# Rotary embedding over eight batches: batch 3's store on sync, another share of TensorE tiles, a last batch stored in halves

## The chip, the cores and the metric

The kernel runs on one core of a Trainium2 chip. The metric is the device time of one execution in microseconds, as the median of several runs. The profile is one further execution taken by the hardware profiler; its span runs from the core's first instruction to its last, and is a little shorter than the device time.

## The reference

```python
x1 = x[..., : d_head // 2]
x2 = x[..., d_head // 2 :]
out1 = x1 * cos - x2 * sin
out2 = x1 * sin + x2 * cos
return np.concatenate([out1, out2], axis=-1)
```

`x` is 8 batches x 2048 positions x 8 heads x 64 values in float32 (33.55 MB); `cos` and `sin` are 2048 x 32 and shared by batches and heads. Every value of `x` is read once and every result written once, 67 MB in all, for two multiplications and one addition each.

## The kernel before

**Tiling.** A batch is one tile `xt` of 128 partitions x 8192 values: partition q holds 16 consecutive positions of 512 values (H x D). It is loaded as one DMA of 4 MB, in rows of 32 KB, and batch 0 as rows of 8, 8 and 16 KB. Five such tiles are there (`NBUF = 5`); results are written over the input in the same tile, and the tile is stored from there. Batches 0 to 4 are loaded at the start; batch b + 5 is loaded by `load` after batch b has been stored, into the tile that this frees.

**Pieces.** A batch is worked on in four pieces of 2048 values per partition (`UNIT`); the first batch begins with two half pieces, and the last ends with two. Each piece is one call of `rotate`, in one of three kinds, which `kinds` (L98 to L100) sets:
- A (the default): GpSimd makes `t2`, the sin products with halves swapped, in two instructions (L122). VectorE makes `t1 = x * cos` (L129), and adds `t1 + t2` into `xt` (L136).
- B: GpSimd and VectorE make `t2` and `t1` as in A, but TensorE adds them: it multiplies both by the unit matrix `eye` and accumulates in PSUM (L143, L144), in two halves `o`, and ScalarE copies each half into `xt` (L145).
- C: GpSimd has no part. VectorE makes the cos product (L129) and the sin product (L148); TensorE adds or subtracts them by `eye` and `neye` (L160, L161), and ScalarE copies (L165).

Before the change, the first piece of batches 1 and 3 is C, the first of 2, 4 and 5 is B, and all others are A.

**Buffers.** `t2` of A and B pieces comes from a pool of three buffers, `t1` of A pieces from one buffer in PSUM, `t1` of B pieces and both products of C pieces from a pool of two (`t1s`), and `o` from one PSUM buffer. A buffer is used again when its last reader is done: for `t2` that is VectorE's addition in an A piece and TensorE's last matmul in a B piece. Which buffer a tile gets is settled when the program is built.

**Order and queues.** `keep` holds the instructions of each engine in the order of the source. There are two DMA queues in use: loads are issued by sync (SP), stores by scalar (ACT), apart from the last batch, whose stores sync issues after its last load. A queue issues in order, and an issue waits until what it reads is computed or what it overwrites is stored. Batch 0 is stored as rows of 2, 14 and 16 KB, the last batch as rows of 16, 8 and 8 KB (`shares`), and every other batch as one DMA of 4 MB.

Of the kernel before, what the change touches and what calls it, by code (L numbers as in the profile page):

```python
# [10 lines left out]
def kernel(  # L11
# [7 lines left out]
    nc = tc.nc  # L19
# [4 lines left out]
    B, S, H, D = x.shape  # L24
# [5 lines left out]
    UNIT = 4 * HD  # L30
    NBUF = 5
    C = 512
    last = B - 1
# [36 lines left out]
        xts[b] = xt  # L70

    def store(b, lo, n):
        queue = nc.sync if b == last else nc.scalar
        keep(queue.dma_start(out=ov[b, :, lo : lo + n], in_=xts[b][:, lo : lo + n]))

    keep(nc.scalar.dma_start(out=sin_sb, in_=sin_src))
# [19 lines left out]
        return dataclasses.replace(a, ap=[a.ap[0][:], a.ap[1][:], [0, n], a.ap[-1][:]])  # L96

    kinds = {}  # L98
    for b, kind in ((1, "C"), (2, "B"), (3, "C"), (4, "B"), (5, "B")):
        kinds[(b, 0)] = kind  # L100

    def rotate(b, lo, n):
        kind = kinds.get((b, lo), "A")
# [73 lines left out]
    def shares(b):  # L177
        if b == 0:
            return [HD, 7 * HD, 2 * UNIT]
        if b == last:  # L180
            return [2 * UNIT, UNIT, UNIT]
        return [ROW]

    for b in range(B):
        done = 0
        outs = list(spans(shares(b)))
        for lo, n in spans(pieces(b)):
            rotate(b, lo, n)
            done = lo + n
            while outs and sum(outs[0]) <= done:  # L190
                store(b, *outs.pop(0))
        if b + NBUF <= last:
            load(b + NBUF)
# [30 lines left out]
```

## Time and profile before

| | us |
|---|---|
| median of 3 runs (lowest to highest) | 163.42 (163.29 to 163.53) |
| span of the profiled execution | 161.6 |
| VectorE busy | 140.1 (87%) |
| GpSimd busy | 138.9 (86%) |
| TensorE matmul busy | 47.1 (29%) |
| ScalarE busy | 12.8 (8%) |
| moved by DMA | 67.65 MB, 419 GB/s on average |

Of the profile's parts, the 40 slices give each engine's busy share in tenths over 40 equal parts of the span; the DMA row is the mean over the 16 DMA engines, which all queues share. The queue table gives each queue's share of the engines' time: q1 is sync's and q10 is scalar's. The timeline lists instructions with start, duration, engine (PE is TensorE, DVE VectorE, ACT ScalarE, POOL GpSimd, SP sync; a q behind the name marks a DMA issue) and line, and in brackets how long the engine was idle before it and what ended that.

The DMA issues, from the page: what, by which engine, how many, KB each and the median us from issue to landing:

| | count | KB | us to landing |
|---|---|---|---|
| loads by sync | 7 | 4096 | 40.3 |
| stores by scalar | 6 | 4096 | 28.3 |
| last batch's first store by sync | 1 | 2048 | 11.1 |
| last batch's two other stores by sync | 2 | 1024 | 7.5 |

### The profile page before, as it was taken

The page shows a single profiled execution, that of the slowest core. Times are in us where ns is not written, and L with a number is a line of the kernel's source. Part 1 is how long each engine was busy: PE and PEld are TensorE (multiplying, and loading weights), DVE is VectorE, ACT ScalarE, POOL GpSimd, SP SyncE. Part 2 cuts the span into 40 slices and gives each one's busy share as a digit, 9 for nine tenths or more (in the row PEclk, how much of TensorE's full clock was granted, in tenths as well). Part 3 has the DMA queues.
Part 4 walks back from the last instruction along what each step waited for, and adds up shares of the span by engine and source line. Part 5 has one row for each costly group of instructions (what it writes and reads, how often), then busy time and mean ns, then how long its engine had stood idle before and what let it go on. Part 6 is the DMA issues. An engine that isn't in the chain of part 4 may idle for free.

```text
span 161.6 us, 460 instructions
## 1 busy us (share of the span) xinstructions
PE 47.1 (29%) x80; PEld 17.8 (11%) x80; DVE 140.1 (87%) x66; ACT 12.8 (8%) x14; POOL 138.9 (86%) x70
## 2 busy tenths in 40 slices
PE   0000000597209750977039813972000000000000
PEld 0000000143004210322023302330000000000000
DVE  0297999999999999999999999699969999899920
ACT  3300000002200220022000120022000000000000
POOL 1399999999999999976999989997899979999500
PEclk9999999999965997599858995699555555555555
DMA  5999999999999999999999999999999999999995
GB/s 157 419 462 413 424 469 403 394 457 457 410 402 450 442 470 389 454 454 389 470 438 389 471 432 389 462 446 398 446 448 406 430 462 406 430 462 397 414 408 225
DMA packets 3458, 67.65 MB, mean 419 GB/s; under 512 B 384, under 2 KB 384, under 8 KB 768
## 3 DMA queue, kind: packets, MB, share of 16 engines
q1 hardware_dynamic: 2016, 38.01, 55.3%
q10 hardware_dynamic: 1440, 29.62, 42.9%
q14 instruction: 2, 0.02, 0.0%
HBM read 34.08 MB, written 33.55 MB: 419 GB/s over the span
## 4 chain that ended last, share of the span: by engine, by line
DVE 53%; DMA 29%; POOL 9%; issue 5%; DVEq 0%; SPq 0%; POOLq 0%
DVE t L129 28%; DMA xt<-in_x_dram 25%; DVE xt L136 22%; POOL t L122 9%; DMA sin_sb<-in_sin_dram 4%; DVE t L148 3%; DVEq L136 0%; SPq L67 0%; POOLq L122 0%
## 5 line engine op out<-in xcount | busy, mean ns | idle before, releaser
L122 POOL TENSOR_TENSOR t<-xt,sin_sb 128x1024 f32<-128x1024 f32 (+1 forms) x32 | 70.5, 2202 | 12.1 <-DMA xt<-in_x_dram 6.7
L129 DVE TENSOR_TENSOR t<-xt,cos_ps 128x2048 f32<-128x2048 f32 (+1 forms) x34 | 73.4, 2166 | 0.8
L122 POOL TENSOR_TENSOR t<-xt,nsin 128x1024 f32<-128x1024 f32 (+1 forms) x32 | 70.5, 2202 | 0.0
L136 DVE TENSOR_TENSOR xt<-t,t 128x2048 f32<-128x2048 f32 (+1 forms) x29 | 62.2, 2144 | 6.7 <-POOL t L122 4.1
L143 PE MATMUL o<-t,eye 128*128 128x512 f32 x24 | 15.9, 749 | 24.4 <-DVE t L129 21.0
L160 PE MATMUL o<-t,eye 128*128 128x512 f32 x16 | 11.2, 789 | 38.3 <-DVE t L129 36.1
L144 PE MATMUL o<-t,eye 128*128 128x512 f32 x24 | 14.7, 698 | 0.0
L145 ACT COPY xt<-o 128x1024 f32<-128x1024 f32 x6 | 6.1, 1012 | 45.7 <-PE o L144 45.7
L143 PEld LDWEIGHTS o<-t,eye 128*128 128x128 f32 x24 | 5.3, 247 | 33.6 <-issue 27.7
L160 PEld LDWEIGHTS o<-t,eye 128*128 128x128 f32 x16 | 3.7, 256 | 43.8 <-POOL t L122 30.2
L165 ACT COPY xt<-o 128x1024 f32<-128x1024 f32 x4 | 4.0, 1012 | 47.3 <-PE o L161 47.3
L93 DVE COPY cos_ps<-cos_sb 128x512 f32<-128x512 f32 x1 | 0.7, 694 | 7.0 <-DMA cos_sb<-in_cos_dram 7.0
L144 PEld LDWEIGHTS o<-t,eye 128*128 128x128 f32 x24 | 5.4, 227 | 7.4 <-issue 7.4
L161 PE MATMUL o<-t,neye 128*128 128x512 f32 x8 | 6.2, 863 | 0.2 <-DVE t L148 0.2
L148 DVE TENSOR_TENSOR t<-xt,sin_ps 128x2048 f32<-128x2048 f32 x2 | 4.6, 2280 | 0.0
L161 PE MATMUL o<-t,eye 128*128 128x512 f32 x8 | 4.1, 592 | 0.0
L161 PEld LDWEIGHTS o<-t,neye 128*128 128x128 f32 x8 | 1.8, 260 | 4.7 <-issue 3.0
L161 PEld LDWEIGHTS o<-t,eye 128*128 128x128 f32 x8 | 1.5, 190 | 1.9 <-issue 1.9
L90 ACT ACT_TABLE_LOAD x1 | 1.3, 1283 | 1.2 <-PEq L208 1.2
L90 ACT ACTIVATE nsin<-sin_sb 128x512 f32<-128x512 f32 x1 | 0.6, 630 | 4.1 <-DMA sin_sb<-in_sin_dram 4.1
L91 ACT COPY sin_ps<-sin_sb 128x512 f32<-128x512 f32 x1 | 0.6, 579 | 0.0
L80 POOL MEMSET eye<- 128x128 f32 x1 | 0.2, 205 | 0.3 <-POOLq L208 0.3
(6 smaller groups left out, 1.0 us busy)
## 6 DMA issues: line engine op xcount, KB each, us to landing
xt<-in_x_dram SPq DMA_DIRECT2D x7, 4096.0 KB, 40.3
out_dram<-xt ACTq DMA_DIRECT2D x6, 4096.0 KB, 28.3
xt<-in_x_dram SPq DMA_DIRECT2D x2, 1024.0 KB, 6.7
xt<-in_x_dram SPq DMA_DIRECT2D x1, 2048.0 KB, 12.4
out_dram<-xt ACTq DMA_DIRECT2D x1, 2048.0 KB, 25.9
out_dram<-xt SPq DMA_DIRECT2D x1, 2048.0 KB, 11.1
out_dram<-xt SPq DMA_DIRECT2D x2, 1024.0 KB, 7.5
out_dram<-xt ACTq DMA_DIRECT2D x1, 1792.0 KB, 20.8
```

The costliest lines, as they stand in the source:

```text
L90: keep(nc.scalar.mul(nsin, sin_sb, -1.0))
L93: keep(nc.vector.tensor_copy(cos_ps, cos_sb))
L122: nc.gpsimd.tensor_mul(out=t2u[:, :, u, :].rearrange("p (r h) d -> p r h d", h=H), in0=xu[:, :, 1 - u, :].rearrange("p (r h) d -> p r h d" ...
L129: nc.vector.tensor_mul(out=t1.rearrange("p (r k d) -> p r k d", r=nr, d=Dh), in0=xk, in1=rep(cos_ps[:, r0 : r0 + nr, :], 2 * H),)
L136: keep(nc.vector.tensor_add(out=xt, in0=t1, in1=t2))
L143: nc.tensor.matmul(oc, eye, t1[:, cs], start=True, stop=False)
L144: nc.tensor.matmul(oc, eye, t2[:, cs], start=False, stop=True)
L145: keep(nc.scalar.copy(xt[:, 2 * j * C : 2 * (j + 1) * C], o))
L148: nc.vector.tensor_mul(out=t2.rearrange("p (r k d) -> p r k d", r=nr, d=Dh), in0=xk, in1=rep(sin_ps[:, r0 : r0 + nr, :], 2 * H),)
L160: nc.tensor.matmul(oc, eye, t1u[:, gs, u, :], start=True, stop=False)
L161: nc.tensor.matmul(oc, eye if u else neye, t2u[:, gs, 1 - u, :], start=False, stop=True)
L165: nc.scalar.copy(xu[:, :, u, :], o.rearrange("p (g d) -> p g d", d=Dh))
```

## The change

```diff
     def store(b, lo, n):
-        queue = nc.sync if b == last else nc.scalar
+        queue = nc.sync if b in (3, last) else nc.scalar
...
     kinds = {}
-    for b, kind in ((1, "C"), (2, "B"), (3, "C"), (4, "B"), (5, "B")):
-        kinds[(b, 0)] = kind
+    for b, j, kind in (
+        (1, 0, "C"),
+        (2, 0, "C"),
+        (3, 0, "C"),
+        (4, 0, "B"),
+        (4, 2, "B"),
+        (5, 0, "B"),
+        (6, 0, "B"),
+    ):
+        kinds[(b, j * UNIT)] = kind
...
         if b == last:
-            return [2 * UNIT, UNIT, UNIT]
+            return [2 * UNIT, 2 * UNIT]
```

Three things change. Batch 3 is stored by sync; in the order of the source that store stands behind the load of batch 7, which is issued at the end of batch 2, so sync issues load 5, load 6, load 7, store 3 and then the last batch's stores. Seven pieces instead of five go through TensorE: three of kind C (batches 1, 2, 3) and four of kind B (batch 4's first and third, and the first of 5 and 6); batch 2's first piece turns from B to C. The last batch is stored as two DMAs of 16 KB rows; its second half of 2 MB, before two stores of 1 MB, each issued when its own piece was done, is now one store, issued when both are done.

## The prediction

> **What bounds the kernel now.** I read the 40 slices and the queue table first, then the timeline from 83 us on, then stretches around the first and the last transfer.
>
> The page's DMA row and queue table, then the stretches (length, busy time by engine, PE clock, DMA share, GB/s):
>
> ```profile
> DMA  5999999999999999999999999999999999999995
> ...
> q1 hardware_dynamic: 2016, 38.01, 55.3%
> q10 hardware_dynamic: 1440, 29.62, 42.9%
> ```
>
> ```profile
> 0.73:1.73 1.00, 0.00 (x0) 0.00 (x0) 0.00 (x0) 0.56 (x1) 0.49 (x2) 1.00 0.00 0
> 1.73:2.20 0.47, 0.00 (x0) 0.00 (x0) 0.00 (x0) 0.47 (x1) 0.00 (x0) 1.00 1.84 279
> ...
> 155.10:159.40 4.30, 0.00 (x0) 0.00 (x0) 0.00 (x0) 0.00 (x0) 0.00 (x0) 0.50 1.01 427
> 159.40:160.40 1.00, 0.00 (x0) 0.00 (x0) 0.00 (x0) 0.00 (x0) 0.00 (x0) 0.50 0.26 107
> ```
>
> The 16 DMA engines are full from 1.7 us to the last packet at 160.4 us; between them sync's queue (q1) and scalar's (q10) take 98%. So the transfers bound the kernel, and a change can gain only by fewer or shorter packets, and lose only by leaving the engines idle. The stretches also price an issue onto idle engines: the first load is issued at 0.73 and its first packets start between 1.73 and 2.20, so 1.0 us to the first engine and 1.5 us to the last.
>
> The timeline (start, duration, engine, line) shows the other runner, GpSimd with VectorE behind it:
>
> ```profile
> 85.49 2.29 DVE L136 TENSOR_TENSOR xt<-t,t 128x2048 f32<-128x2048 f32 x1
> ...
> 87.86 2.34 POOL L122 TENSOR_TENSOR t<-xt,sin_sb 128x1024 f32<-128x1024 f32 x1
> ...
> 92.36 1.02 PE L144 MATMUL o<-t,eye 128*128 128x512 f32 x2
> ...
> 93.42 1.01 ACT L145 COPY xt<-o 128x1024 f32<-128x1024 f32 x1 [3.79 <-PE o L144]
> 93.61 2.34 POOL L122 TENSOR_TENSOR t<-xt,sin_sb 128x1024 f32<-128x1024 f32 x1 [1.10 <-DMA xt<-in_x_dram]
> ...
> 113.71 2.34 POOL L122 TENSOR_TENSOR t<-xt,sin_sb 128x1024 f32<-128x1024 f32 x1 [1.69 <-DMA xt<-in_x_dram]
> ...
> 133.08 2.33 POOL L122 TENSOR_TENSOR t<-xt,sin_sb 128x1024 f32<-128x1024 f32 x1 [1.09 <-DMA xt<-in_x_dram]
> ...
> 144.77 10.24 SPq L74 DMA_DIRECT2D out_dram<-xt  x3
> ...
> 153.42 1.23 DVE L136 TENSOR_TENSOR xt<-t,t 128x1024 f32<-128x1024 f32 x1
> ```
>
> GpSimd works without a break from load to load and waits only 1.1 to 1.7 us at the head of a batch. Its last result reaches the last store at 154.67 (the third issue of the row at 144.77), and the engines drain at 160.4. So the compute chain is 2.2 us ahead of need: the second last store's packets run until 157.9, so the last could be issued as late as 157.9 - 1.0 = 156.9 before an engine goes idle.
>
> **The change, part by part.**
>
> *Last batch in two 2 MB stores.* By the packet records an 8 KB row takes 309 ns and a 16 KB row 611 ns. The last 2 MB are 16 rows of 8 KB per engine now (4.94 us) and 8 of 16 KB then (4.89): 0.06 us less. But nothing of the last 2 MB can start until both small pieces are done, where today its first half covers the wait for the second. All other transfers end at 160.4 - 4.94 = 155.4; so the last issue must come by 155.4 - 1.0 = 154.4. Each us after that is a us of idle engines.
>
> *Store 3 behind load 7.* SP issues it at about 92.9, right after load 7 (92.59); all it waits for is over by then. Nobody waits for it: loads 5, 6, 7 wait for stores 0, 1, 2. The two stores of batch 7 queue behind it on q1, but by 8 packets per engine, done near 132, when the first of them is 15 us away. q10 is empty from store 2's landing (92.5) until store 4, so loads 6 and 7 get up to double share and land near 104 and 114 to 122 (now 113.6 and 132.9). The engines stay full meanwhile, so this part costs and gains nothing by itself: it takes away GpSimd's waits of 1.69 and 1.09 us if GpSimd can use that. Fewer mixed loads and stores may help a little: 32 KB packets take 1213 ns in pure stretches and 1213 to 1221 on average in mixed ones, so at most 16 x 8 ns = 0.13 us.
>
> *Batch 2's piece as C.* One L148 multiply more on VectorE (2.2 us, as 62.45 to 80.90 for batch 3, 18.45 us, against 46.21 to 62.45 for batch 2, 16.24), 4.6 us less on GpSimd. VectorE reaches batch 4 at 83.1 instead of 80.9. GpSimd's saving buys nothing there: it is ahead already and then waits for load 4 (landed 73.98) as before.
>
> *Two B pieces in batch 4, one in batch 6.* Each takes a 2.3 us addition off VectorE. The price is in the three t2 buffers, which GpSimd fills: a B piece holds its buffer until TensorE has read it, an A piece only until VectorE's addition. The built program assigns the buffers (call them X, Y, Z; B pieces marked *): batch 4 Y* X Z* X, batch 5 Y* X Z X, batch 6 Z* X X Y, batch 7 X Y X Y X. GpSimd's piece is 4.6 us (four in 93.61 to 112.0). The steps, times being starts on GpSimd:
> - Batch 4, last piece: needs X from that batch's second piece, whose addition moves from 85.49-87.78 to 87.70-89.99 with VectorE's 2.2 us. Start 90.05 (was 87.86), end 94.65; VectorE leaves batch 4 at 97.0 (was 97.15).
> - Batch 5, first piece: needs Y, held by TensorE. TensorE's piece ran 83.33 to 93.38 and starts 2.2 later, so ends at 95.5; up to 0.9 more if its faster clock comes late. Start 96.0 instead of 93.61.
> - Batch 5, third piece: needs Z from batch 4's second B piece. TensorE can begin it after the ScalarE copy (93.42 + 1.01 + 2.2 to 3.0, so 96.6 to 97.4); a piece takes 8.5 us at full clock (two halves of 3.7 us, as 89.68 to 93.38, and a copy of 1.06) and 10.05 as the one above: end 105.1 to 107.4. GpSimd could start at 105.2; I take 106.0.
> - Then 110.6, 115.2 (batch 6) and 119.8; load 6 is long in. Batch 6's third piece has the same buffer as its second: it waits for the addition that follows 124.4, ending 126.75. Start 126.8, not 124.4: 2.4 us of plain wait. The third buffer lies idle from here on.
> - Then 131.4, 136.0 (batch 7), 140.6, 145.2, ends 149.8; two half pieces. VectorE adds the third piece at 149.9 to 152.2 and needs 5.18 us more (149.47 to 154.65 now): 157.4.
>
> So GpSimd's twelve pieces from batch 5 on begin 2.4 us later, lose 0.8 and 2.4 us on buffers, and win back 2.8 us of load waits: 2.8 in sum, 2.7 by the steps (154.67 to 157.4). The cover is 154.4, so the engines idle. Last packets end at 157.4 + 1.5 + 4.9 = 163.8 on the latest engine, 3.4 us after 160.4. By the first-engine latency it would be 2.9. I take 3.3.
>
> The Trainium skill, "DMA: Bandwidth & Descriptors", section "Latency and other measured facts", gives some 0.6 us to the first byte on the sync and scalar queues; with it the loss would be 2.5 us as an estimate. This trace has 1.0 to 1.5 us, and that is used.
>
> Span 161.6 + 3.3 = 164.9; the runs' median lies 1.82 above the profiled span (163.42 against 161.6), so 166.7.
>
> **Rivals.**
>
> *No loss (the change as a gain in GpSimd time).* If GpSimd's holds are absent or short, eleven pieces from 93.61 at 4.6 us end at 144.2, plus 7.85 us (146.8 to 154.65 now): last issue 152.1, before 154.4. The engines never idle and the time is 163.42 - 0.06 - 0.1 = 163.3, no change that can be told. It decides below 154.4. For it: GpSimd's load waits, 2.8 us, do go. Against: the holds follow from buffers fixed in the program and from row times; to fall under 154.4, 3.0 of 5.6 us must be wrong. Even then there is hardly a gain, since the engines are full already.
>
> *TensorE stays slow.* PE's matmuls take 592 ns at full clock and 1193 at half. The clock was 1.00 in 86.4 to 96.7, 0.50 to 103.5, and 1.00 again. At half throughout, a half piece takes 8 x 0.855 = 6.9 us, a piece 15 us: batch 5's third piece starts at 85.5 + 15 + 1 + 15 = 116.5, 10.5 us later: 177. Against: TensorE has more to do here, and each piece before reached full clock after 3 to 5 us.
> The Trainium skill's "TensorE: Matmul & The Clock Gate", section "Part 1: The HAM clock gate", says one busy window of some 3.4 us brings full clock and one idle window takes it: the second B piece, right behind the first, would run at full clock throughout. If instead the clock falls at a fixed beat, as 96.7 would be, its end is 107. Both lie in my bounds.
>
> **How the numbers follow.** Bounds: batch 5's start 95.4 to 96.4, third piece 105.2 to 107.4 (106.0 less 0.8, plus 1.4), issue latency 1.0 to 1.5 (0.4 less, 0.1 more): 165.5 to 168.2; I carry the low end to 165.0 for part of a hold missing. Chances: forecast 0.86; no loss 0.06; between the two (a hold missing altogether, 163.8 to 165.0) 0.04; TensorE slow 0.04. Predicted 166.7, range 165.0 to 168.2. A difference under 0.2% (0.33 us) can't be told from none here; faster by more has 0.02, since only 0.2 us of packets can go, the same 0.05, slower 0.93.
>
> **What would show it.** Right: DMA slices under 9 just before the end; a last store issued near 157.4 onto idle queues; GpSimd waiting on VectorE near 124 to 127 and on TensorE near 95; loads 6 and 7 landing early. Wrong: a last issue before 154.4, or unbroken DMA to the end; or TensorE pieces of 15 us.

## The result and the profile after

The changed kernel takes 167.70 us (median of 4 runs, 167.50 to 167.89), the kernel before 163.47 (163.29 to 163.91) beside it: a ratio of 1.0258, 95% interval 1.0244 to 1.0271. The forecast was 166.7 us in a range of 165.0 to 168.2. The profiled execution spans 165.9 us, 4.3 more than before; the forecast had 3.3 more.

The page's DMA row and queue table of the changed kernel:

```profile
DMA  5999998999999999999899999999999999999455
...
q1 hardware_dynamic: 2016, 42.21, 60.3%
q10 hardware_dynamic: 1296, 25.43, 35.7%
```

The bytes are the same, 4.2 MB more of them on sync's queue, but the last three slices stand at 4, 5 and 5, where before only the last of these three fell below 9. The stretches around that place (length, busy time by engine, PE clock, DMA share, GB/s):

```profile
150.00:155.00 5.00, 0.00 (x0) 0.00 (x0) 4.76 (x4) 0.00 (x0) 4.29 (x5) 0.50 0.91 354
155.00:156.50 1.50, 0.00 (x0) 0.00 (x0) 1.47 (x2) 0.00 (x0) 1.06 (x1) 0.50 0.36 153
156.50:158.70 2.20, 0.00 (x0) 0.00 (x0) 2.08 (x2) 0.00 (x0) 0.00 (x0) 0.50 0.00 0
158.70:159.30 0.60, 0.00 (x0) 0.00 (x0) 0.00 (x0) 0.00 (x0) 0.00 (x0) 0.50 0.00 0
159.30:159.90 0.60, 0.00 (x0) 0.00 (x0) 0.00 (x0) 0.00 (x0) 0.00 (x0) 0.50 1.02 437
```

No engine starts a packet between 156.5 and 159.3, while VectorE is still at work. Its last addition ends at 158.7; the last store of 2 MB is issued then and starts some 0.9 us later. Followed engine by engine, the packet records show 3.98 us of idle time on average between first and last packet, where the kernel before has 0.04. That is nearly all of the 4.3 us. Two smaller things nearly cancel: on 14 of the 16 engines the first packet of that batch's first store took 1.28 to 1.69 us (0.61 is usual for 16 KB; why is open), and the latest engine ends only 0.1 us after the median one, where before it was 0.55.

Why VectorE is late stands in the timeline of the changed kernel (start, duration, engine, line; in brackets the idle time before and what ended it):

```profile
87.73 2.29 DVE L144 TENSOR_TENSOR xt<-t,t 128x2048 f32<-128x2048 f32 x1
...
90.11 2.34 POOL L130 TENSOR_TENSOR t<-xt,sin_sb 128x1024 f32<-128x1024 f32 x1 [1.92 <-DVE xt L144]
...
97.08 2.36 POOL L130 TENSOR_TENSOR t<-xt,sin_sb 128x1024 f32<-128x1024 f32 x1 [2.34 <-PE o L152]
...
106.73 2.35 POOL L130 TENSOR_TENSOR t<-xt,sin_sb 128x1024 f32<-128x1024 f32 x1 [0.40 <-PE o L152]
...
125.18 2.29 DVE L144 TENSOR_TENSOR xt<-t,t 128x2048 f32<-128x2048 f32 x1 [2.36 <-POOL t L130]
...
127.55 2.34 POOL L130 TENSOR_TENSOR t<-xt,sin_sb 128x1024 f32<-128x1024 f32 x1 [2.40 <-DVE xt L144]
...
153.58 1.25 POOL L130 TENSOR_TENSOR t<-xt,sin_sb 128x512 f32<-128x512 f32 x1 [0.71 <-DVE xt L144]
...
157.46 1.22 DVE L144 TENSOR_TENSOR xt<-t,t 128x1024 f32<-128x1024 f32 x1
```

From 90 us on, GpSimd waits for no load. It waits for buffers: for VectorE's addition (90.11, 127.55, 153.58) or TensorE's last matmul (97.08, 106.73). At 125.18 to 127.55 the two engines take turns: GpSimd fills a buffer while VectorE waits 2.36 us, then VectorE empties it while GpSimd waits 2.40 us. The table of waits of the changed kernel sums it up (total, times, longest):

```profile
POOL t L130 <- DVE xt L144: 6.8, 4, 2.4
...
POOL t L130 <- DMA xt<-in_x_dram: 5.3, 2, 4.9
...
POOL t L130 <- PE o L152: 2.7, 2, 2.3
```

The 4.9 us for a load lie at batch 4, where GpSimd was further ahead than before (2.3 us of wait there) because batch 2's piece had been taken from it.

### The profile page after: what moved, and what is told of

Read it like the earlier page. It is cut to its first block, busy times and chain, and to the rows that moved or that the text cites. A ratio compares the mean times of both kernels' runs of the same rounds, so it can differ in the third digit from the quotient of the medians.

```text
span 165.9 us, 525 instructions
## 1 busy us (share of the span) xinstructions
PE 65.1 (39%) x112; PEld 24.3 (15%) x112; DVE 137.3 (83%) x65; ACT 16.8 (10%) x18; POOL 134.7 (81%) x68
## 4 chain that ended last, share of the span: by engine, by line
DVE 57%; POOL 19%; issue 7%; PE 7%; DMA 4%; ACT 2%; DVEq 0%; ACTq 0%; POOLq 0%
DVE t L137 30%; DVE xt L144 22%; POOL t L130 19%; DVE t L156 4%; PE o L151 4%; DMA sin_sb<-in_sin_dram 4%; PE o L152 3%; ACT xt L153 2%; DVEq L144 0%; ACTq L153 0%; POOLq L130 0%
## 5 line engine op out<-in xcount | busy, mean ns | idle before, releaser
L130 POOL TENSOR_TENSOR t<-xt,sin_sb 128x1024 f32<-128x1024 f32 (+1 forms) x31 | 68.2, 2198 | 20.8 <-DVE xt L144 6.8
L144 DVE TENSOR_TENSOR xt<-t,t 128x2048 f32<-128x2048 f32 (+1 forms) x27 | 57.6, 2133 | 13.6 <-POOL t L130 11.3
L130 POOL TENSOR_TENSOR t<-xt,nsin 128x1024 f32<-128x1024 f32 (+1 forms) x31 | 68.1, 2197 | 0.0
L168 PE MATMUL o<-t,eye 128*128 128x512 f32 x24 | 17.2, 806 | 47.2 <-POOL t L130 30.2
L151 PE MATMUL o<-t,eye 128*128 128x512 f32 x32 | 20.5, 729 | 19.1 <-DVE t L137 12.3
L152 PE MATMUL o<-t,eye 128*128 128x512 f32 x32 | 18.4, 660 | 0.0
L168 PEld LDWEIGHTS o<-t,eye 128*128 128x128 f32 x24 | 5.4, 250 | 56.0 <-POOL t L130 30.2
L153 ACT COPY xt<-o 128x1024 f32<-128x1024 f32 x8 | 8.1, 1012 | 45.9 <-PE o L152 32.4
L173 ACT COPY xt<-o 128x1024 f32<-128x1024 f32 x6 | 6.1, 1012 | 64.7 <-PE o L169 64.7
L151 PEld LDWEIGHTS o<-t,eye 128*128 128x128 f32 x32 | 6.4, 222 | 30.8 <-issue 18.8
L169 PE MATMUL o<-t,neye 128*128 128x512 f32 x12 | 9.6, 891 | 0.3 <-DVE t L156 0.2
L152 PEld LDWEIGHTS o<-t,eye 128*128 128x128 f32 x32 | 7.1, 222 | 9.7 <-issue 9.7
L156 DVE TENSOR_TENSOR t<-xt,sin_ps 128x2048 f32<-128x2048 f32 x3 | 6.8, 2279 | 0.0
L169 PE MATMUL o<-t,eye 128*128 128x512 f32 x12 | 6.1, 592 | 0.0
L169 PEld LDWEIGHTS o<-t,neye 128*128 128x128 f32 x12 | 3.1, 287 | 7.3 <-issue 4.0
L169 PEld LDWEIGHTS o<-t,eye 128*128 128x128 f32 x12 | 2.3, 190 | 2.9 <-issue 2.9
```

What stands on the lines that cost most here:

```text
L130: nc.gpsimd.tensor_mul(out=t2u[:, :, u, :].rearrange("p (r h) d -> p r h d", h=H), in0=xu[:, :, 1 - u, :].rearrange("p (r h) d -> p r h d" ...
L144: keep(nc.vector.tensor_add(out=xt, in0=t1, in1=t2))
L151: nc.tensor.matmul(oc, eye, t1[:, cs], start=True, stop=False)
L152: nc.tensor.matmul(oc, eye, t2[:, cs], start=False, stop=True)
L153: keep(nc.scalar.copy(xt[:, 2 * j * C : 2 * (j + 1) * C], o))
L156: nc.vector.tensor_mul(out=t2.rearrange("p (r k d) -> p r k d", r=nr, d=Dh), in0=xk, in1=rep(sin_ps[:, r0 : r0 + nr, :], 2 * H),)
```

## The experiments

Each ran in five rounds beside the kernel before, whose median was 163.4 (the change's own row is the result above). "Last issue" is when sync issues the last store; "idle" is the mean idle time of a DMA engine between its first and last packet, and "last packet" the median engine's and the latest engine's end, all from the packet records of one profiled execution each. By-hand means that the t2 buffers are chosen in the source. The profiled execution is not always one of median length: for the halves alone it goes with a run of 164.03 us, for the change by hand with one of 165.64 us, 0.5 and 1.1 us above the times in the table.

| kernel | store 3 | kinds | t2 buffers | last batch | last issue | idle | last packet | time | ratio (95%) |
|---|---|---|---|---|---|---|---|---|---|
| before | scalar | old | built | 16, 8, 8 | 154.67 | 0.04 | 159.84 / 160.39 | 163.4 | 1 |
| changed | sync | new | built | 16, 16 | 158.72 | 3.98 | 164.54 / 164.62 | 167.70 | 1.0258 (1.0244 to 1.0271) |
| three stores | sync | new | built | 16, 8, 8 | 158.04 | 1.26 | 161.46 / 161.55 | 164.53 | 1.0077 (1.0061 to 1.0093) |
| old kinds | sync | old | built | 16, 16 | 153.14 | 0.04 | 159.93 / 160.82 | 163.88 | 1.0029 (1.0014 to 1.0044) |
| store 3 alone | sync | old | built | 16, 8, 8 | 153.43 | 0.05 | 159.84 / 161.41 | 164.01 | 1.0034 (1.0015 to 1.0053) |
| halves alone | scalar | old | built | 16, 16 | 155.05 | 1.14 | 160.89 / 160.98 | 163.54 | 1.0012 (1.0002 to 1.0021) |
| kinds alone | scalar | new | built | 16, 8, 8 | 163.49 | 6.12 | 166.91 / 166.98 | 169.78 | 1.0396 (1.0371 to 1.0422) |
| changed, by hand | sync | new | by hand | 16, 16 | 156.72 | 2.84 | 162.55 / 162.62 | 164.56 | 1.0083 (1.0055 to 1.0111) |
| by hand, three stores | sync | new | by hand | 16, 8, 8 | 155.09 | 0.05 | 159.85 / 160.72 | 163.86 | 1.0034 (1.0022 to 1.0046) |
| kinds alone, by hand | scalar | new | by hand | 16, 8, 8 | 156.41 | 0.24 | 159.87 / 160.97 | 164.16 | 1.0037 (1.0026 to 1.0048) |
| by hand, one B less | sync | new less one | by hand | 16, 16 | 154.19 | 0.45 | 160.02 / 161.14 | 164.06 | 1.0031 (1.0018 to 1.0044) |
| changed, again | sync | new | built | 16, 16 | 157.37 | 3.41 | 163.20 / 163.26 | 167.41 | 1.0232 (1.0211 to 1.0253) |

### Three stores at the end

```diff
-            return [2 * UNIT, 2 * UNIT]
+            return [2 * UNIT, UNIT, UNIT]
```

> The changed kernel with the last batch stored as before (16, 8 and 8 KB rows); the other two edits stay. Theory (late compute chain, then 2 MB that nothing covers): the last issue stays near 158.7 us, but only 1 MB hangs on it; 158.7 + 0.8 to 1.5 + 2.5 = 162.0 to 162.7 for the last packet instead of 164.6, so 165.1 to 165.8. Rival (store 3 on sync is the loss): 167.7 as the change. Rival (the halves alone are the loss): 163.5 as before.

Measured 164.53, 3.2 us below the change with nearly the same late chain (last issue 158.04). The store before it (152.86) carries the engines to 157.7 on average, so they idle 1.26 us and only 1 MB is left. The theory's direction holds and both rivals fall; its 165.1 to 165.8 was too high, since it took the chain to be as late as in the change's profile and up to 1.5 us from issue to packet, where these profiles show some 0.9.

### The old kinds

```diff
-    for b, j, kind in (
...
+    for b, kind in ((1, "C"), (2, "B"), (3, "C"), (4, "B"), (5, "B")):
+        kinds[(b, 0)] = kind
```

> The changed kernel with the piece kinds of before (C in batches 1 and 3, B in 2, 4 and 5); store 3 on sync and the two halves stay. Theory (the t2 buffers held by B pieces make the chain late): GpSimd's holds go and the early loads take its load waits, last issue 152.5 to 154.5, the engines idle for at most 0.8 us: 163.3 to 164.2. Rival (store 3 on sync): 167 or more. Rival (the halves alone): 167.7, as the change.

Measured 163.88, as the theory has it: the last issue falls to 153.14 and the idle time to 0.04 us. The new kinds carry 3.8 of the 4.2 us when the last batch is stored in halves.

### Store 3 on sync, and the two halves, each alone

```diff
-        queue = nc.sync if b == last else nc.scalar
+        queue = nc.sync if b in (3, last) else nc.scalar
```

> The kernel before with store 3 on sync and nothing else. Theory: the DMA engines stay full whichever queue feeds them, 163.2 to 163.5; loads 6 and 7 land some 10 us earlier and the last issue at 152.5 to 154.7. Rival (store 3 on sync holds back the last stores): 165 or more.

```diff
-            return [2 * UNIT, UNIT, UNIT]
+            return [2 * UNIT, 2 * UNIT]
```

> The kernel before with the last batch in two halves and nothing else. Theory: last issue as before at 154.7, the engines drain at 155.4 and start again 0.8 to 1.5 us after the issue, so 0.1 to 0.8 us idle: 163.5 to 164.3. Rival (the halves alone are the loss): 167 to 168.

Store 3 alone: load 7 lands at 124.3 instead of 132.9 and the last issue comes 1.2 us earlier, but the time doesn't fall; 164.01 lies over the theory's 163.2 to 163.5, though far from the rival. The median engine ends at 159.84 as before; only the latest ends 1.0 later. Stretches of the tail with store 3 alone:

```profile
155.00:158.00 3.00, 0.00 (x0) 0.00 (x0) 0.00 (x0) 0.00 (x0) 0.00 (x0) 0.50 1.00 423
158.00:159.50 1.50, 0.00 (x0) 0.00 (x0) 0.00 (x0) 0.00 (x0) 0.00 (x0) 0.50 0.95 404
159.50:160.40 0.90, 0.00 (x0) 0.00 (x0) 0.00 (x0) 0.00 (x0) 0.00 (x0) 0.50 0.29 118
160.40:161.50 1.10, 0.00 (x0) 0.00 (x0) 0.00 (x0) 0.00 (x0) 0.00 (x0) 0.50 0.11 45
```

A share of 0.11 after 160.4 is two engines of sixteen finishing alone (0.00 in the kernel before). Packets of store 4 near 110 and 113 took up to 0.66 us longer than their 1.21. Why just there, this study doesn't settle. Nor need it happen every time: six of the twelve runs took 163.3 to 163.8 us and six 164.2 to 164.6, and the profile is of one of the latter (164.40).

The halves alone cost 0.12% (0.02 to 0.21%), 0.17 us by the medians, in the theory's range of 163.5 to 164.3. The engines do idle, 1.14 us in the profile, which is of the longest of the twelve runs (164.03). Even there the median engine ends 1.05 us later than before but the latest only 0.59: before, the latest engine ended 0.55 after the median one, while after a pause in which all ran dry they start within 0.15 us of each other (155.89 to 156.04) and end so too (160.89 and 160.98). How long the engines idle in a run of median length isn't on record.

### The new kinds alone, with the buffers as built and by hand

```diff
-    for b, kind in ((1, "C"), (2, "B"), (3, "C"), (4, "B"), (5, "B")):
-        kinds[(b, 0)] = kind
+    for b, j, kind in (
...
```

> The kernel before with the new kinds and nothing else (store 3 on scalar, last batch as 16, 8, 8 KB rows). The built program hands out the t2 buffers otherwise than in the change: batches 5 and 6 get the buffer of the piece just before in four places, which is a full wait for VectorE's addition or TensorE's piece each time. Theory (the buffers make the chain late): GpSimd loses another 5 to 6 us, last issue 163 to 164, last packet 166.3 to 167.3: 168.8 to 170.0. Rival (the new kinds cost what TensorE and VectorE have to do, whatever the buffer): as the kernel with three stores at the end and store 3 on sync, 164.5.

Measured 169.78, in the theory's range and worse than the whole change. GpSimd's long waits in the timeline of this kernel:

```profile
97.63 2.35 POOL L130 TENSOR_TENSOR t<-xt,sin_sb 128x1024 f32<-128x1024 f32 x1 [2.40 <-DVE xt L144]
...
109.27 2.33 POOL L130 TENSOR_TENSOR t<-xt,sin_sb 128x1024 f32<-128x1024 f32 x1 [2.40 <-DVE xt L144]
...
130.04 2.34 POOL L130 TENSOR_TENSOR t<-xt,sin_sb 128x1024 f32<-128x1024 f32 x1 [2.40 <-DVE xt L144]
...
137.09 2.32 POOL L130 TENSOR_TENSOR t<-xt,sin_sb 128x1024 f32<-128x1024 f32 x1 [2.40 <-DVE xt L144]
```

Four waits of one addition each, where the whole change has one: the same pieces, another assignment of the buffers, which the build chooses anew when a store moves. (The rival named the kernel with three stores, which has these kinds and that last batch, at 164.53; the two differ in store 3's queue and in the buffers.) The same kernel with the buffers by hand:

```diff
-    t2_pool = ctx.enter_context(tc.tile_pool(name="t2p", bufs=3))
+    t2_pool = ctx.enter_context(tc.tile_pool(name="t2p", bufs=1))
...
+    turn = iter("XZYXZ" "YXZ" "YXZ" "YXZ" "YXZX" "YXZX" "ZXYX" "ZYXZY")
...
-            t2 = t2_pool.tile([P, n], f32, tag="t2")
+            t2 = t2_pool.tile([P, n], f32, tag="t2" + next(turn), name="t2")
```

> The kernel before with the new kinds and the by-hand buffers (store 3 on scalar, three last stores). Theory: 163.3 to 163.9, five to six us below the new kinds with the buffers as built. Rival (buffers don't matter): the same as the new kinds alone.

Measured 164.16, 5.6 us less for nothing but the choice of buffer, and 0.3 over the theory's range. The last issue comes 7.1 us earlier (156.41 after 163.49) with the same work on TensorE and VectorE, so it is the choice of buffers, and not that work, that makes most of the lateness. The 1.7 us that stay against the kernel before go with GpSimd's two remaining waits for TensorE (1.95 and 0.39 us in this profile).

### The change with the buffers by hand

The same edit on the changed kernel; the groups are the batches, and only from batch 6's third piece on does it differ from what is built.

> The change with the same three t2 buffers, each piece's buffer written out by hand: as built up to batch 6's second piece, then the third piece of batch 6 in the buffer that lies idle, and the rest in turn. Nothing else differs. Theory: the 2.4 us before batch 6's third piece and the 0.7 us before the last half piece go; last issue at 156.0 to 156.6, last packet 161.8 to 162.4: 165.0 to 165.7. Rival (buffers don't matter): 167.7.

Measured 164.56, 3.1 us less by the medians. GpSimd's waits from 90 us on in this kernel are these, and no more:

```profile
90.53 2.34 POOL L132 TENSOR_TENSOR t<-xt,sin_sb 128x1024 f32<-128x1024 f32 x1 [2.19 <-DVE xt L146]
...
97.37 2.34 POOL L132 TENSOR_TENSOR t<-xt,sin_sb 128x1024 f32<-128x1024 f32 x1 [2.20 <-PE o L154]
...
107.02 2.35 POOL L132 TENSOR_TENSOR t<-xt,sin_sb 128x1024 f32<-128x1024 f32 x1 [0.42 <-PE o L154]
...
125.42 2.34 POOL L132 TENSOR_TENSOR t<-xt,sin_sb 128x1024 f32<-128x1024 f32 x1
```

Batch 6's third piece starts at 125.42 without a wait, in place of 127.55. The last issue falls by 2.0 us to 156.72 (156.0 to 156.6 were expected). This profile is of a run of 165.64 us, in the theory's 165.0 to 165.7 and 2.0 us below the profiled run of the change (167.65), so the time follows the last issue. Four of the six runs took 164.1 to 164.6 us, below the theory's range, and two 165.6 to 165.7; the last section of experiments shows an execution-to-execution difference of that size, the time at which TensorE's clock rises. With three stores at the end as well:

> The same by-hand buffers, with the last batch stored as 16, 8 and 8 KB rows. Theory: the second last store is issued near 153.8 and keeps the engines busy to 157.9, the last issue at 156.3 comes in time: 163.3 to 163.9, as before the change. Rival (three stores are worth some 3.2 us as they were on the change): 162 to 162.5.

Measured 163.86, in range: a last issue at 155.1 comes in time when 1 MB before it is still moving, and then three stores are worth 0.7 us by the medians, not 3.2. (The chain itself is 1.6 us earlier in this profile than in the one above: TensorE's clock rose at 88.8 us here and at 91.6 there.)

### One B piece less, and the change again

```diff
-        (4, 2, "B"),
...
+    turn = iter("XZYXZ" "YXZ" "YXZ" "YXZ" "YXZX" "ZYXY" "XZYZ" "XYZXY")
```

> The change without batch 4's second B piece (it becomes A), and with a by-hand buffer order that gives batch 5's first piece a buffer that VectorE has freed instead of the one that TensorE holds. Both holds on TensorE in batch 5 (2.3 and 0.4 us) should go, VectorE gets one addition (2.3 us) more. Theory: batch 5 starts on GpSimd near 94.8, the last issue falls from 156.7 (by-hand buffers with the second B piece) to 153.2 to 154.2, before the engines drain: 163.4 to 164.0. Rival (VectorE's load sets the end, TensorE's holds are covered): the last issue stays at 156 to 157 and the time at 164.6 or rises.

Measured 164.06, last issue 154.19: the theory, with 0.1 us over its range. Of GpSimd's two holds on TensorE none is left; batch 5 starts at 95.39 after 0.49 us for VectorE. One addition more on VectorE costs nothing here. The 2.5 us in the last issue are not all due to the edit, though: with the second B piece the two by-hand profiles have it at 156.72, with TensorE's clock rising at 91.6, and at 155.09, with the rise at 88.8. Here it rose at 89.5, so 0.9 us is the fairer figure, and the edit has two parts, the piece and the buffers.

> The changed kernel itself beside it, as a measure on the same chip: 167.4 to 168.0 by every theory.

Measured 167.41 (ratio 1.0232, 1.0211 to 1.0253). Its profile is the more telling result. Stretches of TensorE's first B piece in batch 4, in the first profile of the change and in this one; the column after the five engines is PE's clock:

```profile
83.10:89.90 6.80, 4.33 (x5) 1.85 (x6) 6.70 (x4) 0.00 (x0) 5.08 (x3) 0.50 1.06 458
89.90:96.70 6.80, 5.65 (x12) 2.11 (x10) 6.45 (x4) 1.01 (x1) 4.64 (x2) 0.89 1.01 430
```

```profile
83.10:89.90 6.80, 4.29 (x7) 2.01 (x8) 6.70 (x4) 0.00 (x0) 4.86 (x3) 0.59 1.03 443
89.90:96.70 6.80, 4.60 (x11) 1.51 (x9) 6.46 (x4) 2.02 (x2) 5.60 (x3) 1.00 1.00 425
```

The same piece begins at 85.6 in both, but full clock comes at 91.4 in the first (0.89 of full speed over its second stretch) and at 88.7 in the second (0.59 over its first): 2.7 us more at half clock, which is 1.35 us of work. GpSimd's batch 5 starts at 97.08 there and 95.73 here, and the last issue is 158.72 and 157.37: the same 1.35 us apart. The spans are 165.9 and 164.5 us; the times of these two runs, 167.65 and 167.39, don't show the difference, as the profile is a further execution.

The records of the granted clock in the twelve profiles show where this comes from. From one change of the clock to the next it is always a whole multiple of 3.41 us (in the change's first profile two of them from 47.1 to 53.9, eight from 91.4 to 118.7), and these steps lie differently in each execution. In the first profile a step began at 84.6 and the next at 88.0; TensorE was busy for 2.43 us of the 3.4 between them, and the clock rose only after the step that followed. In the second a step began at 85.3; TensorE was busy for 3.05 us of it, and the clock rose at its end, 88.7.

## Why the prediction was right, and where it was off

**The bound.** Full DMA engines, so that a loss can only be idle engines: right for this change, where 3.98 us of idle time stand against 4.3 us. As a rule it was too narrow: store 3 alone lost 0.34% with 0.05 us of idle time, by engines that ended late.

**The halves.** That only the late chain makes them dear was right: 0.17 us on the kernel before, 3.2 on the change (167.70 against 164.53). The forecast's sharp point of 154.4 was too simple: beyond it, idle time first eats up the unevenness of the engines (1.14 us of it moved the latest engine's end by 0.59).

**Store 3.** Loads 6 and 7 landed at 102.7 and 113.6 (104 and 114 to 122 were forecast), store 3 at 132.9 (near 132), with the engines full, and GpSimd could not use it. That it costs nothing by itself was not quite right: 0.34% alone (0.15 to 0.53%), in the profiled execution from two late engines.

**Batch 2 as C.** VectorE reached batch 4 at 83.15 (83.1), and GpSimd's saving became a longer wait for load 4.

**The buffers.** The step that carries the result; every hold was in its place. Batch 4's last piece 90.11 (forecast 90.05), batch 5's first 97.08 (96.0), its third 106.73 (106.0), batch 6's third 127.55 after 2.40 us (126.8, 2.4), last issue 158.72 (157.4). Two terms were too small. The bound for TensorE's first piece, 95.4 to 96.4, let its faster clock come 0.9 us late at most; here it came 5.8 us after the first matmul (85.57 to 91.4), against 3.1 in the kernel before (83.33 to 86.4), so that nearly the whole first half piece ran at half clock (first copy at 92.23). That cost 1.35 us, of which some 0.7 lay beyond the forecast and stayed. The rest, some 0.6, is the tail: VectorE's multiply and addition take 4.72 us a piece against GpSimd's 4.57, so that from 132 on VectorE falls behind. It adds the third piece of batch 7 from 151.21 on, 0.76 us after GpSimd has made it, where the forecast had 0.1; the last half piece's wait of 0.71 us comes from the same lag. The 5.18 us from there on were right.

**Issue to last packet.** 5.9 us, at the lower of the two priced values (5.9 and 6.4), where the forecast took some 6.3. These 0.4 us hide part of the 1.3 us by which the chain was later than forecast, so that the forecast came as near as 1.0 us partly by luck: two errors offset each other. On another phase of the clock the second profile's last issue, 157.37, all but meets the forecast's 157.4.

**The rivals.** No loss: fell, as the engines did idle. TensorE slow: batch 4's second B piece ran right behind the first at full clock (its halves are copied from 101.88 and from 106.69 on, each 3.8 us after the end of the copy before, as in a piece at full clock). So the Trainium skill's "TensorE: Matmul & The Clock Gate", "Part 1: The HAM clock gate", fits better than a clock that falls at a fixed beat whatever TensorE does: a busy window brings full clock, and it stays while TensorE is busy. It also says the window is free-running; the 3.41 us steps of the clock records, which lie differently in each execution, agree with that, and it accounts for the 1.35 us between the two profiles of one program.

None of the versions beats the kernel before. With the chain in time, all end within 0.4% of it and their median engines at 159.8 to 160.0: the transfers fill the time.

## What to carry to other kernels

Work moved to another engine keeps its buffers as long as that engine takes to read them: count the buffers that are free at each start before you count the saved instructions, and look up which buffer the built program gives to which piece. When transfers fill the time, an earlier chain gains nothing, and a late one costs about the idle time that it leaves, less what the engines' uneven ends take up, so keep the last store small and something in flight before it. An edit that moves a store can change the assignment of buffers elsewhere; single edits then don't add up.

## What was not expected

- Full DMA engines don't end together: the latest ended 0.5 to 1.6 us after the median one in the kernels without idle time, and within 0.1 us after a pause of 1 us or more. The 0.3 to 0.4% that the repaired versions still lose lie there; what delays single engines stays open.
- The time at which TensorE's clock rose, set by steps of 3.41 us that lie differently in each execution, moved the whole chain by 1.35 us between two executions of one program. Compare the ends of two chains from single profiles only with this in mind.
- New kinds alone were worse than the whole change (169.78 against 167.70), by the choice of buffers.
